# A split QKV projection on one core: the rows of the first two pairs dealt to the sixteen transfer engines in turn

## The chip, the cores and the metric

The kernel runs on one core of a Trainium2 chip. The metric is the device time of one execution in microseconds; for the kernel before, the median of three runs is 358.44 us (358.43 to 358.5). One further execution was recorded by the hardware profiler, and all traces and views below are of that one.

## The reference

The input `x` has the shape 16 x 512 x 768, the weight `w_qkv` the shape 768 x 2304, both float32. The output stacks the three column ranges of the product.

```python
def reference(x, w_qkv):
    qkv = np.matmul(x, w_qkv)
    hidden = x.shape[-1]                 # 768
    q = qkv[..., :hidden]
    k = qkv[..., hidden:2*hidden]
    v = qkv[..., 2*hidden:]
    return np.stack([q, k, v], axis=0).astype(np.float32)
```

Seen as one matrix, `x` has 8192 rows of 768 numbers, 3072 bytes each, one behind the other in memory. The output has three such planes of 8192 rows of 3072 bytes.

## The kernel before

**Tiles.** The 8192 rows are worked on in 32 pairs (`NP = 32`), each pair being two tiles of 128 rows. The 2304 columns are two blocks of 1024, numbered q = 0 and 1, and a remainder of 256 columns (`REM`). The contraction over 768 is cut into six steps of 128 (`KT = 6`). From pair 2 on each pair's block is done by the seven products of Strassen's scheme with sums of `x` (`sums_x`) and of the weights (`sum_w`), two of the products in bf16 and five in float32r; the remainder is done plainly (`rem`). The first two pairs, 0 and 1, are done plainly in bf16 (`block`, line 479), since the weight sums are not there yet when they start.

**Two ways for x to come in.** Pairs 2 and up are loaded in pieces of 192 columns (`load_x`, `load_x_rows`; 768 bytes in one piece, 32 partitions to a DMA), and VectorE transposes them in blocks of 32 x 32 (`transpose`, line 153). Pairs 0 and 1 are loaded in whole rows (`load_rows`, line 157), one DMA to a pair: partition m takes row m of the pair's first tile and row m of its second. The rows are then cast to bf16 by VectorE and ScalarE together (`cast_row`, lines 165 and 166), turned by TensorE against an identity matrix (`turn_row`, line 179), and copied from PSUM into the operand tile `xb` (`copy_row`).

**Two tiles to a partition.** The loaded tile `xin` is 128 partitions x 2 x 768. Which row of the pair lies in which partition and half is free, so long as the outputs are written back in the same assignment: a row of `x` becomes a column of the stationary operand and then a partition of the result. `rows_of` (line 293) is the assignment for the outputs: row r * 128 + m of the pair for partition m and half r.

**Order at the start.** Everything is in an order written out by hand. SyncE's queue issues the loads of pair 0 and pair 1 (line 160), then six DMAs of 256 KB and more of weights (line 92, tile `st`), the remainder's weights (`str`), the rows of pair 2 (line 137), and the weights of block q = 1. TensorE does ten dummy products on zeros (`busy(10)`, line 452), turns pair 0, does two more dummies (`busy(2)`), turns pair 1, and then begins the 48 products of `block` for q = 0.

**Stores.** `store_quad` (line 296) writes 128 x 2 x 1024 results of one pair and block in two DMAs, one of 768 KB and one of 256 KB, in pieces of 3072 and 1024 bytes; `rem` (line 313) writes the remainder's 128 x 2 x 256 results in one DMA of 256 KB. All of them go through SyncE's queue. The stores of pairs 0 and 1 are ten DMAs: two of remainders after the weights of q = 1, four after the loads of pair 3, and four after the end of `block(1, 1)`.

Of the kernel before, what the change touches and what calls it, by code (L numbers as in the profile page):

```python
# [10 lines left out]
def kernel(  # L11
# [20 lines left out]
    nc = tc.nc  # L32
    P = 128
    G = 32
    B, T, H = x.shape
# [4 lines left out]
    KH = KT // 2  # L40
    KC = K // 4
    NP = M // (2 * P)
    CB = 512
    REM = N3 - 4 * CB
    Q_OFF = (0, 2 * CB + REM)
    R_OFF = 2 * CB
    fp32 = mybir.dt.float32
# [7 lines left out]
    out_flat = out.rearrange("s b t h -> s (b t) h")  # L55
# [21 lines left out]

    b1 = [w_pool.tile([P, KT, CB], bf16, name=f"b1_{q}") for q in range(2)]
    b22 = [w_pool.tile([P, KH, CB], f32r, name=f"b22_{q}") for q in range(2)]
    t_0 = w_pool.tile([P, 4, KH, CB], f32r, name="t_0")  # L80
    w_rem[1] = rem_pool.tile([P, KH, REM], bf16, name="w_rem1")
# [39 lines left out]
    xin, xf, xb, sr = {}, {}, {}, {}  # L121
# [19 lines left out]
    def load_x(p, other):  # L141
        xin[p] = xin_pool.tile([P, 2 * P // G, KC], fp32, name="xin")
        load_x_half(p, 0, nc.sync)
        if other is not None:
            load_x_half(p, 1, other)

    def transpose(p, cuts=(0, 8)):
        if p not in xf:
            xf[p] = xf_pool.tile([P, KT, 2 * P], fp32, name="xf")
        turned = xf[p][:].rearrange("p j (g b) -> p g j b", b=G)  # L150
        rows = xin[p][:].rearrange("p g (a j) -> p g j a", a=G)
        for g, end in zip(cuts, cuts[1:]):
            nc.vector.transpose(turned[:, g:end], rows[:, g:end])  # L153

    def load_rows(p):
        xin[p] = xin_pool.tile([P, 2, K], fp32, name="xin")
        rows = x_flat[p * 2 * P:(p + 1) * 2 * P, :]
        nc.sync.dma_start(xin[p][:], rows.rearrange("(r m) k -> m r k", m=P))  # L160

    xc, turned_rows = {}, {}

# [63 lines left out]
    def quad(p, q, pool=o_pool, tag="o"):  # L227
        u = Quad()
        u.p, u.q = p, q
        u.o = pool.tile([P, 2, 2 * CB], fp32, name="o", tag=tag)  # L230
        u.x = u.y = u.z = None
        return u

    def product(u, n, ps, start):
        t1, t2, t3, t4 = ts[u.q]
        if n <= 2:
            h = (n - 1) * KH
            lhs = [xb[u.p][:, h + j, :P] for j in range(KH)]
            rhs = [b1[u.q][:, h + j, :] for j in range(KH)]
        else:  # L240
            k, t = {3: (4, b22[u.q][:]), 4: (0, t4), 5: (1, t1), 6: (2, t2), 7: (3, t3)}[n]
            lhs = [sr[u.p][:, k, j, :] for j in range(KH)]
            rhs = [t[:, j, :] for j in range(KH)]
        for j in range(KH):
            nc.tensor.matmul(  # L245
                ps[:], lhs[j], rhs[j],
                start=(start and j == 0), stop=(j == KH - 1), skip_group_check=True,
            )
# [7 lines left out]
    def do(u, n, out=True):  # L256
# [17 lines left out]
        elif n == 5:  # L274
            u.y = bank()
            product(u, 5, u.y, True)
            if u.p == NP - 1:
                nc.scalar.activation(c22, u.y[:], ident)
        elif n == 7:
            product(u, 7, u.x, False)  # L280
            if u.p == NP - 1:
                nc.vector.tensor_tensor(c22, c22, u.x[:], op=add)
# [7 lines left out]
            product(u, 3, u.y, False)  # L290
            nc.vector.tensor_tensor(c12, c12, u.y[:], op=add)  # L291

    def rows_of(s, p, lo, hi):
        return out_flat[s, p * 2 * P:(p + 1) * 2 * P, lo:hi].rearrange("(r m) n -> m r n", m=P)

    def store_quad(u):
        if u.q == 0:
            nc.sync.dma_start(rows_of(0, u.p, 0, H), u.o[:, :, :H])
            nc.sync.dma_start(rows_of(1, u.p, 0, 2 * CB - H), u.o[:, :, H:])
        else:  # L300
            part = 2 * H - Q_OFF[1]
            nc.sync.dma_start(rows_of(1, u.p, H - part, H), u.o[:, :, :part])
            nc.sync.dma_start(rows_of(2, u.p, 0, H), u.o[:, :, part:])


    def rem_row(p, r, ps):
        for j in range(KT):
            nc.tensor.matmul(  # L308
                ps, xb[p][:, j, r * P:(r + 1) * P], w_rem[j // KH][:, j % KH, :],
                start=(j == 0), stop=(j == KT - 1), skip_group_check=True,  # L310
            )

    def rem(p, eng=nc.sync, between=None):
        ps = ps_pool.tile([P, 2, REM], fp32, name="ps")
        rem_row(p, 0, ps[:, 0, :])
        if between is not None:
            between()
        rem_row(p, 1, ps[:, 1, :])

        def copied():  # L320
            o = or_pool.tile([P, 2, REM], fp32, name="orem")
            act.activation(o[:], ps[:], ident)  # L322
            return lambda: eng.dma_start(rows_of(1, p, R_OFF - H, R_OFF - H + REM), o[:])

        return copied

    def two(a, b, early, u=None):

        do(a, 1)
        do(b, 1, u is None)  # L330
        if u is None:
            early()
            rem(a.p)()()
        else:
            middle(u)
            copied = rem(a.p, between=lambda: third(u))
            evacuate(b)
            early()
            copied()()
            fourth(u)  # L340
            load_x(a.p + 3, nc.sync)
        do(a, 2)
        do(b, 2)
        summed(a, b)

    def summed(a, b, between={}, store=True):

        parts = {7: (1, CB, 2 * CB), 4: (1, 0, CB), 3: (0, CB, 2 * CB)}
        for i, (u, n) in enumerate(
            ((a, 6), (b, 6), (a, 5), (a, 7), (b, 5), (b, 7), (a, 4), (a, 3), (b, 4), (b, 3))  # L350
        ):
            do(u, n)
            if store == "parts" and n in parts:
                store_cols(u, *parts[n], nc.sync)
            elif n == 3 and store:
                store_quad(u)
            between.get(i, lambda: None)()
# [9 lines left out]
    def add_second(u):  # L367
        product(u, 2, u.z, False)
        act.activation(u.o[:, 0, :CB], u.z[:], ident)  # L369
        store_quad(u)  # L370

    def plain(a, b, c, d, early, rem_c, stored=False):

        add_first(a)
        add_first(b)
        rem(a.p)()()
        do(c, 1)
        do(d, 1)
        early()
        rem_c()  # L380
        do(c, 2)
        do(d, 2)
        add_second(a)
        add_second(b)
        if stored:
            for u in (c, d):
                store_cols(u, 0, 0, CB, nc.sync)
# [43 lines left out]
        rem_stored(a.p, 1, 2, lambda dst, src: act.activation(dst, src, ident), act)  # L431


    ND = 2
    zero = xb_pool.tile([P, CB], bf16, name="zero", tag="xb")
    nc.vector.memset(zero[:], 0.0)
    load_rows(0)
    nc.scalar.activation(tiny[:], zero[:, :1], ident)
    make_identity(nc, eye)
    load_rows(1)  # L440
    load_blocks(0, 0, 1)
    load_blocks(0, 1)
# [62 lines left out]
    def fourth(u):  # L505
        do(u, 4)
        store_quad(u)

    def ahead(p, reversed_pair):
        transpose(p)  # L510
        if reversed_pair:
            sums_x(p)
            round_x(p)
        else:
            round_x(p)
            sums_x(p)
# [58 lines left out]
    u = quad(2, 0)  # L575
# [55 lines left out]
    def load_next(p, other):  # L631
        if p < NP:
            load_x(p, other)

    def early():
        ahead(ND + 2, False)
        load_x(ND + 3, nc.sync)

    two(quad(ND + 1, 0), quad(ND + 1, 1), early, u2)

    def early():
        ahead(ND + 3, True)
        load_x(ND + 5, nc.sync)

    two(quad(ND + 2, 0), quad(ND + 2, 1), early)
    transpose(ND + 4, (0, 4))

    for p in range(ND + 3, NP - 1, 2):
        first = p == ND + 3
# [6 lines left out]
        def early():  # L656
            ahead(p + 2, p + 2 < NP - 1)
            load_next(p + 4, nc.scalar)
# [6 lines left out]
        c, d = quad(p + 1, 0), quad(p + 1, 1)  # L665
        final = p + 3 >= NP
        plain(a, b, c, d, early, lambda: rem(c.p)()(), final)
# [32 lines left out]
```

## Time and profile before

| | |
|---|---|
| median of the runs | 358.44 us (358.43 to 358.5) |
| the profiled execution's own time | 358.38 us |
| its span in the profile | 356.6 us |
| granted TensorE clock | 1.0 throughout |
| TensorE busy | 351.8 us (99%) |
| VectorE, ScalarE, GpSimd busy | 264.4, 186.2 and 177.7 us |
| moved by the DMA engines | 108.10 MB, mean 303 GB/s |
| read from and written to the main memory | 32.24 MB and 75.50 MB |

The span runs from the first recorded instruction to the last; the execution's own time holds 1.78 us more, which lie around it. Names in the profile: PE is TensorE, PEld its weight loads, DVE VectorE, ACT ScalarE, POOL GpSimd, and SPq the queue of SyncE, which issues nearly all DMAs. A line such as `xin<-in_x_dram` is a DMA from the tensor `x` into the tile `xin`.

### The profile page before, as it was taken

How to read it: one execution, taken by the hardware profiler on the slowest of the kernel's cores; microseconds unless marked ns; L12 is line 12 of the kernel's file. 1: busy time of each engine (PE TensorE's matmuls, PEld its weight loads, DVE VectorE, ACT ScalarE, POOL GpSimd, SP SyncE). 2: the span in 40 equal slices, each digit the busy share in tenths (PEclk: the TensorE clock that was granted, in tenths of full speed). 3: DMA queues.
4: the chain of work that ended last, by engine and by line, in shares of the span. 5: the costliest groups of instructions: out<-in, count | busy, mean ns of one | idle time of the engine just before them, and what ended most of it. 6: DMA issues, size and time to landing. Idle time of an engine off the chain costs nothing.

```text
span 356.6 us, 5348 instructions
## 1 busy us (share of the span) xinstructions
PE 351.8 (99%) x1782; PEld 252.1 (71%) x1782; DVE 264.4 (74%) x309; ACT 186.2 (52%) x321; POOL 177.7 (50%) x184
## 2 busy tenths in 40 slices
PE   8999999999999999999999999999999999999996
PEld 3474677768677686877768677686877768777675
DVE  3799876796877869777695877869777695876743
ACT  5588655445454553645545454553645545454553
POOL 0121773376566453666535566353665535566320
PEclk9999999999999999999999999999999999999999
DMA  7997999999999898998979899798999979887397
GB/s 297 379 359 259 336 367 352 368 313 361 280 339 313 244 368 213 351 254 292 359 178 399 226 337 313 242 372 206 350 267 300 333 192 396 227 290 297 149 380 267
DMA packets 82076, 108.10 MB, mean 303 GB/s; under 512 B 4993, under 2 KB 62081, under 8 KB 82049
## 3 DMA queue, kind: packets, MB, share of 16 engines
q1 hardware_dynamic: 75376, 102.91, 86.3%
q10 hardware_dynamic: 6672, 4.85, 5.1%
q8 instruction: 14, 0.23, 0.3%
q14 instruction: 14, 0.11, 0.1%
HBM read 32.24 MB, written 75.50 MB: 302 GB/s over the span
## 4 chain that ended last, share of the span: by engine, by line
PE 97%; DMA 2%; ACT 0%; SPq 0%; issue 0%
PE ps L245 79%; PE ps L308 11%; PE ps L479 6%; DMA xin<-in_x_dram 2%; PE ps L412 0%; PE ps L179 0%; ACT xc L166 0%; SPq L160 0%; ACT orem L431 0%
## 5 line engine op out<-in xcount | busy, mean ns | idle before, releaser
L245 PE MATMUL ps<-t,s 128*128 128x512 f32 x720 | 178.0, 395 | 0.0
L245 PEld LDWEIGHTS ps<-t,s 128*128 128x128 f32 x720 | 135.0, 188 | 29.6
L153 DVE STREAM_TRANSPOSE xf<-xin 128x768 f32<-128x768 f32 (+2 forms) x46 | 93.4, 2035 | 2.2 <-DMA xin<-in_x_dram 2.2
L245 PE MATMUL ps<-b,xb 128*128 128x512 bf16 x360 | 85.2, 379 | 0.0
L285 DVE TENSOR_TENSOR o<-o,ps 128x512 f32<-128x512 f32 x56 | 38.5, 688 | 52.3 <-ACT o L284 52.3
L192 POOL CAST xb<-xf 128x1536 bf16<-128x1536 f32 x28 | 41.1, 1468 | 57.4 <-DVE xf L153 57.4
L212 POOL TENSOR_TENSOR s<-xf 128x384 fp32r<-128x384 f32 x29 | 31.0, 1069 | 72.2 <-DVE xf L153 70.5
L245 PEld LDWEIGHTS <-xb 128*128 128x128 bf16 x360 | 33.9, 98 | 36.9 <-issue 4.2
L291 DVE TENSOR_TENSOR o<-o,ps 128x512 f32<-128x512 f32 x60 | 41.2, 688 | 20.6 <-PE ps L245 19.5
L284 ACT ACTIVATE o<-ps 128x512 f32<-128x512 f32 x56 | 33.5, 598 | 42.0 <-PE ps L245 42.0
L245 PE MATMUL ps<-b,s 128*128 128x512 f32 x180 | 50.6, 389 | 0.0
L288 ACT ACTIVATE o<-ps 128x512 f32<-128x512 f32 x60 | 35.9, 598 | 25.2 <-PE ps L245 22.7
L365 DVE TENSOR_TENSOR o<-o,ps 128x512 f32<-128x512 f32 x78 | 47.8, 683 | 0.0
L273 ACT ACTIVATE o<-ps 128x512 f32<-128x512 f32 x60 | 36.1, 601 | 19.1 <-PE ps L245 15.4
L308 PE MATMUL ps<-w_rem,xb 128*128 128x256 bf16 x372 | 45.7, 273 | 0.0
L322 ACT ACTIVATE orem<-ps 128x512 f32<-128x512 f32 x31 | 18.5, 597 | 49.1 <-PE ps L308 28.6
L308 PEld LDWEIGHTS <-xb 128*128 128x128 bf16 x372 | 36.2, 98 | 10.9 <-issue 0.5
L245 PEld LDWEIGHTS ps<-b,s 128*128 128x128 f32 x180 | 33.8, 188 | 7.0
L213 POOL TENSOR_TENSOR s<-s,xf 128x384 fp32r<-128x384 f32 x29 | 29.6, 1021 | 2.3
L214 POOL TENSOR_TENSOR s<-xf 128x384 fp32r<-128x384 f32 x29 | 29.5, 1018 | 0.0
L216 POOL TENSOR_TENSOR s<-xf,s 128x384 fp32r<-128x384 f32 x29 | 29.4, 1012 | 0.0
L369 ACT ACTIVATE o<-ps 128x512 f32<-128x512 f32 x26 | 15.6, 599 | 16.7 <-PE ps L245 16.0
(53 smaller groups left out, 165.7 us busy)
## 6 DMA issues: line engine op xcount, KB each, us to landing
out_dram<-o SPq DMA_DIRECT2D x60, 768.0 KB, 4.6
out_dram<-o SPq DMA_DIRECT2D x76, 256.0 KB, 3.8
xin<-in_x_dram SPq DMA_DIRECT2D x88, 192.0 KB, 5.7
out_dram<-orem SPq DMA_DIRECT2D x31, 256.0 KB, 2.4
xin<-in_x_dram ACTq DMA_DIRECT2D x24, 192.0 KB, 4.3
st<-in_w_qkv_dram SPq DMA_DIRECT2D x5, 768.0 KB, 7.7
xin<-in_x_dram SPq DMA_DIRECT2D x2, 768.0 KB, 4.9
st<-in_w_qkv_dram SPq DMA_DIRECT2D x6, 256.0 KB, 5.9
```

Of the source, the lines that this page charges most:

```text
L153: nc.vector.transpose(turned[:, g:end], rows[:, g:end])
L192: nc.gpsimd.tensor_copy(out=xb[p][:], in_=xf[p][:])
L212: 1: lambda g: g.tensor_tensor(s[:, 1], a21, a22, op=add),
L213: 2: lambda g: g.tensor_tensor(s[:, 2], s[:, 1], a11, op=sub),
L245: nc.tensor.matmul(ps[:], lhs[j], rhs[j], start=(start and j == 0), stop=(j == KH - 1), skip_group_check=True,)
L273: nc.scalar.activation(c12, u.x[:], ident)
L284: nc.scalar.activation(c22, u.x[:], ident)
L285: nc.vector.tensor_tensor(c22, c22, u.y[:], op=add)
L288: nc.scalar.activation(c21, u.x[:], ident)
L291: nc.vector.tensor_tensor(c12, c12, u.y[:], op=add)
L308: nc.tensor.matmul(ps, xb[p][:, j, r * P:(r + 1) * P], w_rem[j // KH][:, j % KH, :], start=(j == 0), stop=(j == KT - 1), skip_group_check= ...
L365: dve.tensor_tensor(c, c, u.z[:], op=add)
```

## The change

A function `dealt` views the 256 rows of a pair as 16 rows of 16: row 16 n + e stands at place (e, n). `load_rows` reads the rows in this order, and the stores of pairs 0 and 1 write in it; `rows_of` becomes `store_rows`, which issues the DMA itself and takes the old order for all other pairs. The order in which the 16 x 16 rows are named runs over e outside and n inside, and fills partitions 0 to 127 with two rows each. So partitions 8 e to 8 e + 7 hold rows e, e + 16, e + 32 and so on, where they held rows 8 e to 8 e + 7 of either tile. If each of the sixteen transfer engines serves eight partitions next to each other, then at its n-th row engine e reads row 16 n + e, 3 KB beside that of its neighbour, where it read rows 24 KB from its neighbour's. No instruction is added or removed, and the order on every engine and queue is as before.

```diff
+    ND = 2
...
+    def dealt(rows):
+        return rows.rearrange("(n e) k -> e n k", e=16)
+
     def load_rows(p):
         xin[p] = xin_pool.tile([P, 2, K], fp32, name="xin")
         rows = x_flat[p * 2 * P:(p + 1) * 2 * P, :]
-        nc.sync.dma_start(xin[p][:], rows.rearrange("(r m) k -> m r k", m=P))
+        nc.sync.dma_start(xin[p][:], dealt(rows))
...
-    def rows_of(s, p, lo, hi):
-        return out_flat[s, p * 2 * P:(p + 1) * 2 * P, lo:hi].rearrange("(r m) n -> m r n", m=P)
+    def store_rows(s, p, lo, hi, src, eng=nc.sync):
+        rows = out_flat[s, p * 2 * P:(p + 1) * 2 * P, lo:hi]
+        if p < ND:
+            eng.dma_start(dealt(rows), src)
+        else:
+            eng.dma_start(rows.rearrange("(r m) n -> m r n", m=P), src)
...
-            nc.sync.dma_start(rows_of(0, u.p, 0, H), u.o[:, :, :H])
-            nc.sync.dma_start(rows_of(1, u.p, 0, 2 * CB - H), u.o[:, :, H:])
+            store_rows(0, u.p, 0, H, u.o[:, :, :H])
+            store_rows(1, u.p, 0, 2 * CB - H, u.o[:, :, H:])
...
-            nc.sync.dma_start(rows_of(1, u.p, H - part, H), u.o[:, :, :part])
-            nc.sync.dma_start(rows_of(2, u.p, 0, H), u.o[:, :, part:])
+            store_rows(1, u.p, H - part, H, u.o[:, :, :part])
+            store_rows(2, u.p, 0, H, u.o[:, :, part:])
...
-            return lambda: eng.dma_start(rows_of(1, p, R_OFF - H, R_OFF - H + REM), o[:])
+            return lambda: store_rows(1, p, R_OFF - H, R_OFF - H + REM, o[:], eng)
...
-    ND = 2
```

## The prediction

> **What bounds the kernel now.** I read the page first, then the chain that ended last, then the timeline of the first ten microseconds, then the DMA rates there. From the page:
>
> ```profile
> span 356.6 us, 5348 instructions
> PE 351.8 (99%) x1782; PEld 252.1 (71%) x1782; DVE 264.4 (74%) x309; ACT 186.2 (52%) x321; POOL 177.7 (50%) x184
> PE 97%; DMA 2%; ACT 0%; SPq 0%; issue 0%
> ```
>
> TensorE is busy for all but 4.8 us. The chain (start, length, what) shows where the 2% of DMA stands:
>
> ```profile
> 0.74 0.44 SPq L160
> 1.24 5.57 DMA xin<-in_x_dram
> 6.84 0.45 ACT xc L166
> 7.39 0.85 PE ps L179 x12
> 8.24 10.36 PE ps L479 x48
> ...
> 352.14 1.35 PE ps L412 x18
> 353.52 0.28 ACT orem L431
> ```
>
> The load of pair 1, issued at 1.24, lands 5.57 us later at 6.81. Cast, turn and first product follow at once, and from 8.24 to 353.5 the chain never leaves TensorE. So the change can reach the end in two ways only: the first product begins at another time, or something it delays later makes TensorE wait. The timeline (start, length, engine, line, instruction, idle before) shows how tight the first step is:
>
> ```profile
> 4.95 0.63 DVE L165 CAST xc<-xin 128x384 bf16<-128x384 f32 x2 [3.82 <-DMA xin<-in_x_dram]
> 5.53 0.95 PE L179 MATMUL ps<-eye,xc 128*128 128x128 bf16 x12
> 6.32 0.59 PE L452 MATMUL ps<-zero 128*128 128x512 bf16 x2
> 6.84 0.78 ACT L166 ACTIVATE xc<-xin 128x288 bf16<-128x288 f32 x2 [0.95 <-DMA xin<-in_x_dram]
> 7.39 0.85 PE L179 MATMUL ps<-eye,xc 128*128 128x128 bf16 x12 [0.48 <-ACT xc L166]
> 7.52 0.31 DVE L165 CAST b<-st 128x288 bf16<-128x288 f32 x1
> ```
>
> The DMA rates from 1 to 7 us, in 40 slices of 0.15 us, are these:
>
> ```profile
> GB/s 0 0 0 0 0 143 225 102 20 61 102 348 328 389 471 410 369 410 471 410 348 492 451 369 369 430 430 369 430 471 369 369 492 437 341 403 382 396 423 410
> ```
>
> Three phases: the first rows at 1.83 us, a hole from 2.05 to 2.65, then about 410 GB/s without a break.
>
> **The change part by part.** No instruction is added, removed or moved; twelve DMAs name other rows: two loads and ten stores.
>
> *The loads' steady part.* In the trace's packet records the two loads are 512 packets of 3072 bytes, 32 to each of 16 engines. All but a few take 119 to 121 ns and follow each other at 117.7 ns. The weights behind them come from rows of 9216 bytes, six to a partition, so eight partitions are 432 KB apart in place of 24, and they too run at 404 to 410 GB/s (from 7 us on). Distance does not show in the rate; I put this part at nothing.
>
> *The loads' start.* This is all that is left. 32 packets of 0.1177 us are 3.77 us; from the first start at 1.83 that would end at 5.60, and the last packet ends at 6.52, so 0.92 us go at the start. Part is the engines' staggered start (1.83 to about 2.1), part the hole. Eight packets took 0.32 to 0.82 us in place of 0.12; summed over the 512, the excess over 0.121 is 5.2 us, 0.33 per engine. The delayed packets, whenever they began, end together between 2.47 and 2.83: that looks like a latency met by all engines at the beginning, more than engines in each other's way. The nearest row for neighbouring rows supports this. From pair 2 on, x comes in 768-byte pieces, 32 partitions to a DMA, so two neighbouring rows to an engine and 6 KB from engine to engine. At 118.74 us such a load starts after the stores, and the rates from 118 to 121 us, in slices of 0.075 us, are:
>
> ```profile
> GB/s 341 369 382 396 369 355 396 205 41 38 75 92 20 61 41 20 31 41 10 31 102 195 205 297 297 246 328 287 266 297 297 348 338 348 410 348 307 297 277 256
> ```
>
> The hole is there again, longer, and its packets take up to 0.93 us. From first packet to full rate it is 0.82 us in the first load and about 0.9 here. Rows close together do not take it away. I take 0 for it. The ends: if the whole hole went, the last packet could end at 2.1 + 3.77 = 5.87, 0.65 earlier; if a hole like that at 118.7 came in place of the present one, 0.1 to 0.4 later (excess per engine over the usual time there: 0.37 to 0.72 us against 0.33), and twice that if pair 1's load met one of its own, 0.8.
>
> *What a shift is worth.* A later landing of pair 1 costs its full size: ScalarE and VectorE cast 0.03 us after it, and the weights behind it in the same queues (first step landing near 7.5, cast at 7.52) shift alike. An earlier one is capped. The ten dummies hold TensorE until 5.5 and the two others until 6.91, while the turn of pair 1 begins at 7.36: 0.45 us to win, and about 0.1 more if pair 0's turn runs without its wait. So at most 0.55, less than 0.72 us, which is 0.2% and about what a measurement of this kernel can tell from no change.
>
> *Issue.* The two loads take 0.44 us each on the queue; other DMAs here take 0.31 to 0.68. If the uneven shapes (16 x 16 rows against 128 x 2) cost as much as the longest, the first packet comes 0.24 later; if the least, 0.13 earlier; pair 1's issue hides behind pair 0's packets. I take 0, since the number of pieces is the same.
>
> *The stores.* Ten DMAs, 4.72 MB, issued between 21 and 46 us. 3072-byte packets there take 121 to 124 ns, as the loads' do. I take no change; no row has sixteen engines writing side by side, so the price of a slower store is a rival below. If they were faster nothing is won, for TensorE waits for no DMA then. What covers them: x of pairs 4 and 5 is queued behind them. VectorE waits 1.79 us for pair 5 and transposes it at 55.75; GpSimd has its second sum ready at 61.04, and TensorE wants it at 63.81. That is 2.77 us of cover. The first remainder store also holds a buffer that ScalarE gets at 31.67; the casts behind it are wanted at 35.0 and the first is done at 33.2, 1.8 us of cover, while all 16 of its packets on an engine last 16 x 46 ns = 0.74 us.
>
> The sum: 356.6 + 0 of span, and 1.78 around it, 358.38; the median of the runs stands 0.06 above. Forecast 358.4.
>
> **The rivals.** *The hole shrinks* (0.20). [...] Against it stand the hole at 118.7 and the weights' undisturbed rate. Gain 0.1 to 0.55, likeliest 0.3: 358.1. [...]
>
> *The hole grows* (0.24). Sixteen engines open the same 48 KB at once and then all move on together; the 6 KB rows of the later loads have the larger excess. It decides from the first tenth of a microsecond on, because nothing covers pair 1's landing. 0.1 to 0.8 from the row above, up to 1.0 with a slow issue: 358.5 to 359.4, likeliest 358.9.
>
> *The dealt stores write slower* (0.10). Sixteen writers in one stretch of 48 KB could wait for each other. 4.72 MB at about 390 GB/s are 12.1 us; the cover of 2.77 us is gone when they take 23% longer. Then pair 5's sums are late and TensorE waits at 63.8: at half as long again, 6.0 - 2.8 = 3.2 us, 361.6. Nothing in the profile speaks for it but the lack of a row.
>
> *The engines do not get neighbouring rows* (inside the forecast's 0.46). If an engine does not serve eight partitions next to each other, the rows of one moment are other ones, and the loads run as before: 358.4. The trace names no partition for a packet. [...]
>
> **How the numbers follow.** Forecast 0.46, 358.2 to 358.6. The low end takes in most of the shrinking hole, 357.9; the high end the growing one, 359.5. Left out are the slower stores (0.10), some of the growing hole (0.05) and 0.03 below. Faster by over 0.2% (under 357.72) needs more than the cap of 0.55, a step I have not seen: 0.04. Slower (over 359.16): the stores with 0.09, the upper part of the growing hole and of the issue with 0.15, 0.02 for waits not named: 0.26. Within: 0.70.
>
> **What would show it.** Right: pair 1's load lands within 0.15 us of 6.81, the first product at 8.1 to 8.4, the hole again near 0.6 us, 3072-byte packets at 121 ns, TensorE idle still 4.8 us. The shrinking hole: rates over 300 before 2.5 us, and two dummies followed at once by pair 1's turn. The growing hole: casts later than 6.95 and everything shifted by that. Slower stores: VectorE's wait for pair 5 over 4 us and a gap on TensorE near 64. Wrong altogether would be a time under 357.8, or a wait of TensorE between 9 and 50 us.

## The result, and the profile after

The changed kernel takes 364.36 us, median of 6 runs (362.9 to 364.97), against 358.47 us before in the same session: a ratio of 1.0155, 95% interval 1.0136 to 1.0174. It is 5.9 us slower. The profiled execution took 364.43 us, its span 362.6.

The page, with the lines that answer to those of before and the granted clock in 40 slices:

```profile
span 362.6 us, 5329 instructions
...
PE 353.3 (97%) x1763; PEld 253.2 (70%) x1782; DVE 262.3 (72%) x309; ACT 186.6 (51%) x321; POOL 177.3 (49%) x184
...
PEclk9699999999999999999999999999999999999999
```

TensorE has 9.3 us without work, 4.5 more than before, and in the second slice, 9 to 18 us, its clock fell. The first is where the loss begins, the second adds to it. The timeline (start, length, engine, line, instruction, idle before), first the two halves of the first block in the kernel before:

```profile
8.08 5.34 PE L479 MATMUL ps<-b,xb 128*128 128x512 bf16 x24
13.26 5.34 PE L479 MATMUL ps<-both,xb 128*128 128x512 bf16 x24
```

Then the changed kernel:

```profile
6.80 0.63 DVE L169 CAST xc<-xin 128x384 bf16<-128x384 f32 x2 [5.67 <-DMA xin<-in_x_dram]
...
7.38 0.95 PE L183 MATMUL ps<-eye,xc 128*128 128x128 bf16 x12 [1.75 <-ACT xc L170]
...
8.17 0.59 PE L459 MATMUL ps<-zero 128*128 128x512 bf16 x2
...
10.24 0.78 ACT L170 ACTIVATE xc<-xin 128x288 bf16<-128x288 f32 x2 [2.51 <-DMA xin<-in_x_dram]
...
10.80 1.45 PE L183 MATMUL ps<-eye,xc 128*128 128x128 bf16 x12 [2.04 <-ACT xc L170]
...
12.05 7.42 PE L486 MATMUL ps<-b,xb 128*128 128x512 bf16 x23
19.31 5.34 PE L486 MATMUL ps<-both,xb 128*128 128x512 bf16 x24
```

Pair 1 is cast from 10.24 instead of 6.84: 3.40 us. From there to the first product it takes 1.81 us instead of 1.24, because the turn runs 1.45 us instead of 0.85: 0.57 more. And from the first product to the second block it takes 19.31 - 12.05 = 7.26 us instead of 13.26 - 8.08 = 5.18: 2.08 more. The sum is 6.05; the span grew by 6.0. After 19.31 nothing is added.

The clock by stages (window, TensorE busy, and after POOL's busy time the granted clock, DMA share and GB/s):

```profile
7.00:9.00 2.00, 1.38 (x14) 0.87 (x14) 0.79 (x3) 0.74 (x2) 0.00 (x0) 1.00 1.03 223
9.00:11.00 2.00, 0.20 (x3) 0.23 (x4) 0.76 (x3) 0.76 (x3) 0.00 (x0) 0.61 1.04 329
11.00:13.00 2.00, 2.00 (x15) 1.44 (x14) 1.17 (x5) 1.65 (x6) 0.00 (x0) 0.50 1.05 404
13.00:15.00 2.00, 2.00 (x6) 0.64 (x5) 1.24 (x4) 0.91 (x3) 0.00 (x0) 0.50 1.05 408
```

TensorE waits from 8.76 to 10.80 us and comes back at half its clock, which costs the 0.57 and the 2.08 us above, 2.65 together. The same between the places where the clock changes:

```profile
6.01:9.42 3.41, 1.38 (x14) 0.87 (x14) 0.98 (x3) 0.94 (x2) 0.00 (x0) 1.00 1.04 225
9.43:12.83 3.40, 2.03 (x14) 1.58 (x15) 1.75 (x7) 2.23 (x7) 0.00 (x0) 0.50 1.04 385
12.84:16.24 3.40, 3.40 (x9) 1.18 (x8) 1.93 (x7) 1.60 (x4) 0.00 (x0) 0.50 1.06 410
```

The clock falls at 9.42, when TensorE has been waiting for only 0.66 us. Behind it lie 3.41 us of full clock in which it worked 1.38: most of the wait of 1.75 us for pair 0 is in them too. The half clock lasts twice 3.41 us, from 9.42 to 16.25, and the second time TensorE was at work throughout. How little work makes the clock fall, and what brings it back, is not shown here, nor what decides where the stretch of 3.41 us begins. The runs of the changed kernel lie up to 2.1 us apart, those of before 0.4.

Ahead of the first change on record, at 6.01 us here and 5.38 in the kernel before, the views show 1.00 as well. But there the ten dummies take 0.44 us each, against 0.22 for a product of the first block before, so they ran at about half speed: the "1.0 throughout" of the kernel before holds from 5.4 us on.

And the late landing itself. The DMA rates from 1 to 11 us, in slices of 0.25 us:

```profile
GB/s 0 0 0 0 49 147 61 332 381 381 197 209 209 258 283 221 197 197 221 234 258 270 197 221 209 221 209 283 233 221 209 197 201 229 238 328 393 410 402 434
```

The hole at the start is the old one. Three slices come near the full rate; from 3.5 us the two loads run at little over half of it, to the end of their last packet at 9.31; with the weights the rate is back at 393 by 10 us. In the packet records the median 3072-byte packet takes 231 ns in place of 121, and 370 of 512 are over 200. In most half microseconds nearly all packets are at 230 to 250 ns, and every 1.5 to 2 us there is one in which some are back near 160.

The 3.40 us of the landing have three parts. The first packet starts 0.40 us later (2.23 against 1.83). From there to the end of the last packet it takes 7.08 us in place of 4.69, 2.39 more. And the landing follows that end by 0.91 us in place of 0.30, 0.61 more. This last part is there in every run below whose 16 x 16 rows are loaded at half rate (0.65 to 1.05 us, against 0.30 to 0.36 where the packets of 3072 bytes take 121 ns); what holds the landing back is not shown.

### The profile page after: what moved, and what is told of

Its sections match the earlier page's. It is cut to its first block, busy times and chain, and to the rows that moved or that the text cites. A ratio compares the mean times of both kernels' runs of the same rounds, so it can differ in the third digit from the quotient of the medians.

```text
span 362.6 us, 5329 instructions
## 1 busy us (share of the span) xinstructions
PE 353.3 (97%) x1763; PEld 253.2 (70%) x1782; DVE 262.3 (72%) x309; ACT 186.6 (51%) x321; POOL 177.3 (49%) x184
## 4 chain that ended last, share of the span: by engine, by line
PE 73%; POOL 15%; DVE 6%; issue 2%; DMA 2%; ACT 0%; SPq 0%
PE ps L249 55%; PE ps L316 11%; PE ps L486 6%; DVE xf L154 5%; POOL xb L196 5%; POOL s L217 3%; POOL s L216 3%; POOL s L218 3%; DMA xin<-in_x_dram 2%; PE ps L183 0%; PE ps L420 0%; DVE o L295 0%; SPq L164 0%; ACT xc L170 0%; ACT orem L439 0%
## 5 line engine op out<-in xcount | busy, mean ns | idle before, releaser
L249 PE MATMUL ps<-b,xb 128*128 128x512 bf16 x343 | 81.4, 379 | 1.1
```

The source lines that it names most:

```text
L249: nc.tensor.matmul(ps[:], lhs[j], rhs[j], start=(start and j == 0), stop=(j == KH - 1), skip_group_check=True,)
```

## The experiments

Theories at the outset: sixteen engines in one stretch of memory get in each other's way (theory of the memory); the 16 x 16 rows divide the transfer among the engines in a way that makes them meet when they write the tile (theory of the division); uneven shapes are turned into pieces more slowly. In the diffs below the unchanged line is that of the kernel named.

**Loads or stores.** Two halves of the change. First the loads alone (in the changed kernel `if p < 0:` in place of `if p < ND:` in `store_rows`).

> Only the two loads are dealt; the ten stores are as before, so the results of pairs 0 and 1 stand in other rows. Load theory (the dealt loads run at half rate, 231 ns for 3072 bytes in place of 121, and everything follows from that): 364.4 us as with the whole change, pair 1 lands at about 10.2 us. Store theory (part of the 5.9 us is the dealt stores): under 363.

364.19 us, ratio 1.0159 (1.0144 to 1.0174). Pair 1 lands near 9.8 us, the median packet takes 229 ns. The loads alone cost as much as the whole.

Then the stores alone (`load_rows` as before).

> Only the ten stores are dealt, the loads are as before, so the results of pairs 0 and 1 stand in other rows. Load theory: 358.4 us, within 0.3, although 3072-byte store packets may take 200 ns and more. Store theory: over 359.5.

361.73 us, ratio 1.0094 (1.0069 to 1.0119): a miss for the load theory. The loads run at 121 ns again, and TensorE starts as before. But the stores' 3072-byte packets between 32 and 37 us take 220 ns in the median, and the loads of pair 5 behind them land late. VectorE in the kernel before and in this run, and TensorE in this run:

```profile
55.75 3.04 DVE L153 STREAM_TRANSPOSE xf<-xin 128x1536 f32<-128x1536 f32 x1 [1.79 <-DMA xin<-in_x_dram]
```

```profile
59.80 3.02 DVE L154 STREAM_TRANSPOSE xf<-xin 128x1536 f32<-128x1536 f32 x1 [5.43 <-DMA xin<-in_x_dram]
```

```profile
57.20 5.13 PE L249 MATMUL ps<-t,s 128*128 128x512 f32 x21
64.73 1.53 PE L249 MATMUL ps<-b,s 128*128 128x512 f32 x3 [2.40 <-DVE o L289]
```

VectorE's wait for pair 5 is 5.43 us, not 1.79; the additions behind it, which free PSUM, come late, and TensorE waits 2.40 us at 62.3. The clock falls there too:

```profile
62.00:64.00 2.00, 0.34 (x2) 0.00 (x0) 2.00 (x4) 0.89 (x2) 1.00 (x1) 1.00 0.97 245
64.00:66.00 2.00, 1.27 (x3) 1.07 (x4) 1.18 (x2) 0.00 (x0) 1.96 (x3) 0.71 1.08 325
66.00:68.00 2.00, 2.00 (x6) 1.55 (x5) 0.69 (x1) 0.42 (x1) 2.00 (x4) 0.50 1.06 399
```

In the 3.41 us up to the fall at 64.82 TensorE had worked 1.01. Two of the four runs have such a fall (363.05 and 362.13 us, mean clock 0.995), two have not (360.8 and 361.33 us, mean clock 1.0). So the change has two costs, 5.8 and 3.3 us, which do not add up: with both, pair 5 lands 4.4 us later than before (60.0 against 55.6), but TensorE wants it 6.1 us later (69.87 against 63.81), and the stores' loss is covered by the loads'.

**Clock or weights.** The whole change with more dummies:

```diff
-    busy(10)
+    busy(18)
...
-    busy(2)
+    busy(12)
```

> The whole change with eighteen and twelve dummies in place of ten and two, so that TensorE has no idle time before pair 1 lands at about 10.2. Theory (3.4 us of the loss are the late landing, 2.6 us are TensorE's halved clock after its idle time, in pair 1's turn and the first block): the granted clock stays 1.0 and the time is 361.8 us. Rival (the first block is slow for want of weights, not for the clock): 364.4 us.

362.57 us, ratio 1.0117 (1.0100 to 1.0134), the clock 1.0 from 3.8 us on. Pair 1 lands at 10.2 as in the changed kernel, but TensorE's timeline is now this:

```profile
10.77 0.85 PE L183 MATMUL ps<-eye,xc 128*128 128x128 bf16 x12 [0.23 <-ACT xc L170]
11.45 5.34 PE L486 MATMUL ps<-b,xb 128*128 128x512 bf16 x23
16.63 5.34 PE L486 MATMUL ps<-both,xb 128*128 128x512 bf16 x24
```

TensorE begins 3.37 us late and its first block takes 5.18 us again: it was the clock. The time is 0.8 over what I expected, as TensorE is now early enough to meet the late stores: it waits for VectorE at 65.3, and stands 4.0 late behind it in place of 3.4. The same dummies with only the loads dealt take that away:

> Only the loads dealt, with eighteen and twelve dummies in place of ten and two, so that TensorE's clock is kept and the stores stay as before; the results of pairs 0 and 1 stand in other rows. Theory (the loads cost their late landing and the halved clock after it, and nothing else): pair 1 lands near 9.9 in place of 6.8, clock 1.0, 361.3 to 361.8 us. Rival (slower loads cost something more later): over 362.3.

362.29 us, ratio 1.0103 (1.0088 to 1.0118). That is above the range I gave, which rested on a landing at 9.9, and at the edge of the rival's 362.3; in the profiled execution the landing came later:

```profile
1.50 8.96 DMA xin<-in_x_dram
10.45 0.02 issue
10.47 0.45 ACT xc L170
```

That is 3.65 us after the 6.81 of before, and its span, 360.2 us, is 3.6 longer. In this execution the landing's delay goes to the end one for one and, with the clock kept, nothing else does.

**Why the loads run at half rate.** The shape of the change with rows far apart:

```diff
-        nc.sync.dma_start(xin[p][:], rows.rearrange("(r m) k -> m r k", m=P))
+        row = x_flat[p:p + 1, :]
+        far = bass.AP(row.tensor, row.offset, [[32 * K, 16], [2 * K, 16], [1, K]])
+        nc.sync.dma_start(xin[p][:], far)
```

> Loads with the shape of the change (16 x 16 rows against 128 x 2) but with rows far apart: engine e reads rows 32 e + 2 n, 96 KB from its neighbour; pairs 0 and 1 are so computed from other rows of x, the stores are as before. Theory of the memory (sixteen engines in one stretch of 48 KB get in each other's way): 121 ns a packet, 358.4 us. [...]

359.68 us, ratio 1.0039 (1.0025 to 1.0054); the packets take 121 ns. The theories of the division and of uneven shapes had 230 ns and 364.4 us here. So this spoke for the memory, until I saw that 32 rows are sixteen times 2 rows, so that the pattern is one even run of 256 rows and need not be divided by 16. It does settle one thing: the issues took 0.66 and 0.59 us in place of 0.44, nearly as in the change (0.72 and 0.59), and the rate was full, so a longer issue alone does not halve it.

The shape of before with near places (`[[K // 4, P], [32 * K, 2], [1, K]]`):

> Loads with the shape of before (128 x 2 rows on both sides) but with near places: partition p reads 3072 bytes from 768 p on, so that engines stand 3 or 6 KB apart and all read within 96 KB; the pieces overlap, and pairs 0 and 1 are computed from them, the stores are as before. Theory of the memory: 200 ns a packet or more, 362 us or more. Theories of the division and of uneven shapes: 121 ns, pair 1 lands near 6.8, 358.4 us.

359.19 us, ratio 1.0023 (1.0013 to 1.0032), the median packet 121 ns, nine in ten within 149. Sixteen engines within 96 KB run at nearly the full rate. Then three patterns of 16 x 16 that can't be one run, with the distance between engines and the engine's own step near or far (`[[1 * K, 16], [2 * K, 16], [1, K]]`, then 19 and 16, then 33 and 2):

> Loads with the shape of the change; engine e reads rows e + 2 n: neighbours 3 KB apart, its own next row 6 KB on, so all sixteen stay within 48 KB that moves on by 6 KB; rows are read by several engines, pairs 0 and 1 are computed from other rows, the stores are as before. Theory of the neighbours (sixteen engines in one 48 KB stretch slow each other): 200 ns a packet or more, 362 us or more. Theory of the engine's own step (48 KB from a row to its next is what is slow): 121 ns, 359 to 360 us.

> Loads with the shape of the change; engine e reads rows 19 e + 16 n: neighbours 57 KB apart, its own next row 48 KB on as in the change; pairs 0 and 1 are computed from other rows, the stores are as before. Theory of the neighbours: 121 ns a packet, 359 to 360 us. Theory of the engine's own step: 230 ns, 364 us.

> As e3, with 33 rows from engine to engine in place of 32: 32 is sixteen times the step of 2 inside, so that the 16 x 16 rows of e3 were one run of 256 rows at an even step and could be divided like 128 x 2; with 33 they can't. Pairs 0 and 1 are computed from other rows, the stores are as before. Theory of the division: 230 ns a packet, pair 1 lands near 10.2, 363 to 364.5 us. Rival (e3 was fast because its rows are far apart and its own step short): 121 ns, 359.7 us as e3.

363.46 us, 364.61 us and 363.73 us, ratios 1.0136 (1.0115 to 1.0156), 1.0168 (1.0147 to 1.0188) and 1.0143 (1.0122 to 1.0163). The median packet takes 229, 229 and 218 ns. Near or far, short step or long, all are at half rate: the rows don't matter, the 16 x 16 does. e12 differs from e3 in 33 for 32 only. (The view of e8 shows a clock of 1.00 throughout, but its record begins only at 16.89 us, and the first block takes 7.50 us: the half clock is there too.)

Now the other side: the rows of before, even shapes, but 64 partitions to a DMA.

```diff
-        rows = x_flat[p * 2 * P:(p + 1) * 2 * P, :]
-        nc.sync.dma_start(xin[p][:], rows.rearrange("(r m) k -> m r k", m=P))
+        rows = x_flat[p * 2 * P:(p + 1) * 2 * P, :].rearrange("(r m) k -> m r k", m=P)
+        for h in range(2):
+            nc.sync.dma_start(xin[p][h * 64:(h + 1) * 64], rows[h * 64:(h + 1) * 64])
```

> Each load of a pair in two DMAs of 64 partitions, even shapes on both sides, rows as before, results as before. [...] Theory of the memory: 121 ns, 358.4 to 359 us.

363.63 us, ratio 1.0140 (1.0120 to 1.0160), 235 ns a packet (the theory of the division had 231 ns and over 362 us), and the same picture of rates:

```profile
GB/s 0 0 0 0 0 86 49 344 406 332 221 197 209 209 270 246 233 209 197 221 197 270 246 221 221 197 209 209 270 233 221 233 172 201 205 213 352 402 401 402
```

No row moved, and the loss is nearly the same: this speaks for the partitions that are written at one time. The last run issues the upper 64 partitions on ScalarE's queue beside the lower ones on SyncE's (`(nc.sync, nc.scalar)[h].dma_start`, both pairs' loads first):

> As e5, two DMAs of 64 partitions to a pair, but the upper 64 partitions are issued on ScalarE's queue at the same time, and both loads ahead of ScalarE's first instruction; results as before. If each engine alternates between the queues, the lower and the upper 64 partitions are written at one time. [...] Rival (a transfer divided from 64 or 16 is slow in itself, whatever is written beside it): near 230 GB/s as in e5, pair 1 lands near 10, 363 us or more.

364.50 us, ratio 1.0165 (1.0139 to 1.0190). If it is the partitions written at one time that count, I had expected near 400 GB/s and 358 to 359 us: the time goes against that, the course within the run for it. Three windows (TensorE, PEld, VectorE, ScalarE and GpSimd busy, clock, DMA share, GB/s):

```profile
3.50:5.00 1.50, 1.50 (x4) 0.44 (x3) 0.00 (x0) 0.15 (x1) 0.00 (x0) 1.00 1.04 406
5.50:7.00 1.50, 0.28 (x3) 0.16 (x3) 0.63 (x2) 0.73 (x2) 0.00 (x0) 1.00 1.04 219
7.00:8.00 1.00, 1.00 (x14) 0.72 (x13) 0.36 (x1) 0.21 (x1) 0.00 (x0) 1.00 1.04 235
```

From 3.5 to 5.0 us the packet records hold about 100 packets of each queue, 121 ns in the median: both halves of the tile are written, at 406 GB/s. From 5.0 on the queues have come apart. First only ScalarE's packets start, then, from about 6.5, only SyncE's, one half of the tile at a time. ScalarE's 58 packets from 5.0 to 5.5 us still take 134 ns in the median, as the first slices of the change's loads were fast too; behind them it is 237, and the rate is 219 to 235. Same rows, same shapes; which partitions are written beside each other differs. What parted the queues isn't shown, nor why the first half microsecond of a half alone is nearly at the full rate.

I read this as the division: naming the transfer as 16 runs, or in halves of 64 partitions, changes which partitions the engines write at one time, and that sets the rate. This is my inference: a packet's partition is in no trace, nor is an engine's list of partitions, and so the neighbouring partitions to an engine that the prediction starts from are an assumption too. Measured here: 197 to 270 GB/s in all slices of e5 above from 3.5 to 9 us. Two things stay open: the dealt stores' 1024-byte packets kept their 46 ns, and no run dealt the stores' rows apart from their division, as e7, e8 and e12 did for the loads.

**A version that keeps the even shape.** Rows 2 m and 2 m + 1 in partition m, for loads and stores (`dealt` returns `rows.rearrange("(m r) k -> m r k", r=2)`), so that the pair is read in one sweep:

> Loads and stores of pairs 0 and 1 with rows 2 m and 2 m + 1 in partition m: shapes 128 x 2 on both sides, results right, and the engines' rows nearer in all (the whole pair is read in one sweep). Theory of the division: even shapes keep the full rate, 358.4 us; if a partition's two rows become one piece of 6144 bytes, up to 0.2 less. Theory of the neighbours: slower by the share of rows that lie near.

358.79 us, ratio 1.0005 (0.9995 to 1.0014): the same as before. From 3.25 us to the landing at 7.0 the loads run at 336 to 516 GB/s, slice by slice. No version here beats the kernel before.

## Why the prediction was wrong

- **What bounds the kernel** was right. Pair 1's landing decides the start, and from then on nothing in the loads' path covers a delay: 3.65 us of it in e14 are 3.6 us of span.
- **The step that failed is the loads' steady part**, put at nothing because distance between rows does not show in the rate. In these runs that held (e7, e8 and e12 are alike, at 229, 229 and 218 ns a packet), but distance was not the only thing that the edit changed. I read it as a new choice of rows and took the tile's side for unchanged, since the tile's pattern was. The outer count of the memory's side went from 128 to 16, and with it, as I read the runs, the division among engines. Measured for the two loads of 768 KB: 2.39 us more from the first packet to the end of the last, which puts the time outside my range on this term alone, and 0.61 us more from there to the landing, a wait that the sum did not have. The rival on the engines' partitions doubted where the rows would lie and concluded that the loads run as before; it should have asked which partitions would be written together.
- **What a shift is worth** held for the landing and missed its echo, which the sum left out without a reason: TensorE's clock fell after 3.41 us in which it had worked 1.38, and 2.65 us came on top, 44% of the loss in the profiled execution. The profile of before gave a hint: its dummies keep TensorE at work up to the landings.
- **The loads' start**: 0 forecast, and the hole stayed much as it was. The shrinking and the growing hole did not happen. What makes the hole is shown by no run, and the 0.20 for its shrinking was an estimate. With the shape of before and near places (e4) no slice of 0.25 us after the first packet was under 184 GB/s; with rows far apart (e3) the five from 2.0 to 3.25 us were at 0 to 123.
- **Issue**: 0.24 us was my upper end. The two issues took 0.72 and 0.59 us in place of 0.44, and the first packet started at 2.23 instead of 1.83, 0.40 later. The mechanism was right, the size short.
- **The stores**: put at no change, with a rival at 0.10. In e2 the rival's chain came as told, up to VectorE's wait for pair 5 (5.43 us; I had said over 4) and TensorE's near 64, but through VectorE's late additions rather than the late sums alone. Whether the reason is the sixteen writers in one stretch was not tested for the stores; for the loads near rows were not the reason (near rows at 121 ns in e4, far ones at 218 in e12). In the whole change its price was nothing, since TensorE ran later still.
- Slower by over 0.2% had 0.26. The mechanisms that I listed for it were the wrong ones, except for the stores' in e2.

## What to carry to other kernels

Here the access pattern decided more than which bytes move. A load ran at about half rate (218 to 235 ns for 3072 bytes in place of 121) when the memory's side was named as 16 x 16 rows that form no single run, or when a DMA held 64 partitions; with 128 on both sides it ran at or near the full rate, with rows far apart (121 ns, before) and near (121 ns in e4, 336 to 516 GB/s in e13). Look at the rate while the transfer runs, not only at distances in memory. Where TensorE waits for a first load, price the wait together with the clock that it loses (2.65 us here), and count all its waits of the last few microseconds (3.41 here, with 1.38 of work), not the last one alone.

## What the runs showed of the hardware that was not expected

- 128 x 2 rows from a 16 x 16 pattern, and equally from DMAs of 64 partitions, took 218 to 235 ns per 3072 bytes in the median instead of 121; two queues writing both halves of the tile at once ran at 121 ns and 406 GB/s (e15, 3.5 to 5.0 us).
- A 16 x 16 pattern whose two steps form one run (32 rows and 2 rows) kept the full rate, 121 ns a packet in e3; with 33 rows in place of 32 it was 218 ns (e12).
- In seven traces (the changed kernel, e1, e2, e5, e7, e12, e15) the granted clock fell to 0.5 at the end of 3.41 us in which TensorE had worked 0.73 to 1.39 us. In e3 it had worked 1.78 of such 3.41 us (4.16 to 7.57), with single waits of 1.63 and 0.70 us, and the clock stayed at 1.0. The half clock lasted 3.41 us in e2, in the middle of a busy kernel, and 6.83 in the others.
- Where that stretch fell goes with the time: the half clock ended at 14.1 to 14.7 us in e5, e7 and e12 (363.23 to 363.88 us for these executions) and at 16.1 to 16.2 in the changed kernel, e1 and e15 (364.03 to 364.43), though pair 1 landed latest of all in e12, at 10.69.
